# Key cache rows by VectorE block transposes, delta heads in four couples, and ScalarE row statistics in a hybrid decoder layer

## The chip, the core and the metric

One core of one Trainium2 chip runs the program. The metric is device microseconds for one execution, lower is better. TensorE is called PE here, VectorE DVE, ScalarE ACT, GpSimd POOL, and SyncE SP; all DMAs are issued from SP.

## The reference, cut to what matters

One inference step of a one-layer decoder runs over 512 prompt tokens and over 8 sequences of 4 sample tokens, 544 rows in all, width 1024. The rows are scaled and shifted by a condition, multiplied with one wide matrix (11,280 columns), and go through two branches: dilated softmax attention (three groups of eight heads of 64) and a gated delta rule (eight heads of 128, chunks). The branch outputs are gated, merged, multiplied with `w_out`, and normalised per row. The new key and value rows are outputs too.

```python
gate, (qa, ka, va, za, qkv_b, zb, a_b, b_b, ga, gb) = layer_front(x, c, w_cond, b_cond, w_in)
for gi, (window, dil) in enumerate(A_GROUPS):        # ((128,1),(512,4),(2048,16))
    o, l = dilated_prompt(qa[:, :, gi], ka[:, :, gi], va[:, :, gi], window, dil, biases[gi])
    kv_new.append(jnp.stack([ka[:, :, gi], va[:, :, gi]], axis=2)[:, seq - min(window, seq):])
state, o_b = delta_branch(qkv_ext, a_b, b_b, state0, conv_w, a_log, dt_bias)
r = (ALPHA * x + gate[:, None] * (merged @ w_out)).astype(jnp.float32)
mu = jnp.mean(r, axis=-1, keepdims=True)
var = jnp.mean(jnp.square(r - mu), axis=-1, keepdims=True)
return ((r - mu) * lax.rsqrt(var + LN_EPS)).astype(dtype) * ln_g + ln_b
```

## The kernel before, in words

Products are computed at high precision from two rounded parts of each factor: a weight tile `wt` of 128 columns is split into `hi` (ACT, a copy with rounding) and `lo` (DVE, the difference), and so is the input (`hhi`, `hlo`). Each product takes three matmuls per slice of 128 features, so a job of one weight tile is 2 halves x 8 slices x 3 = 48 matmuls of 128x272. These are the groups `pp<-hhi,hi`, `pp<-hhi,lo` and `pp<-hlo,hi`, and `stream` (line 1041) issues them job after job. The list `jobs` (from line 2152) holds the order: for each of four head pairs `j` nine attention jobs (q, k and v of three groups `g`), then jobs of the delta heads (`conv_job`), then the gates `za`, `zb`, `gb`, `ga`.

Everything else on PE is placed between those matmuls. The program does not write its engine queues by hand: a recorder notes each operation with a rank, and `schedule` orders each engine's queue with a cost table and data dependencies. All operations are issued from one line of `emit`, which is why every row of the profile says L727. Each engine works through its queue in order.

The places that the change and the prediction's steps touch:

- `shape_constants` (line 79) packs constant tables. `cst` is the first of them: the 128x128 identity used for PE transposes, a selector `selc`/`selg`, and two masks. Its DMA stands second after the first weights of the condition product (`cond_block`), which uses only the selector.
- `prompt_attention` (from line 1563) waits for q, k and v of one (j, g). It turns v into rows `vrow` by four PE transposes (`pg<-cst,spare`), and k into rows by four more (`pg<-cst,k`; one for g = 0). A copy by ACT takes k's rows from PSUM into a tile of the two-buffer tag `spare`, and DMAs with packets of 512 bytes store them to `out_kv_p`. The layout of k in SBUF is feature by time; in groups 1 and 2 time is stored in an order (r, a, n) of the dilation.
- `TOGETHER` (line 42) groups delta heads. For one group, `delta_blocks` inverts 16x16 blocks by a loop of small DVE operations (`tmp`, `Tb`), and `delta_rule` merges them up to 128x128 with six rounds of small matmuls on parts of the PE array (32x32 and 64x64). The inversion issues as many DVE instructions for one head as for two, and each round visits PE once per group. Before, head 0 and head 7 are groups of their own.
- `sample_prep` starts when head 7's convolution is done and contains one long DVE reciprocal, `kq`.
- At the end four token tiles `tt` of 128 rows are multiplied with `w_out` in two column halves `n`. DVE scales the product (`r<-pp,gp`), adds the residual (`r<-r,xr`), and takes row statistics with `bn_stats` and `bn_aggr`; `norm_out` (line 2332) then subtracts the mean and multiplies with the gain (`r<-r,mv,lng`), takes a reciprocal, and applies the factor and the offset (`r<-r,mv,lnb`, twice).

Of the kernel before, what the change touches and what calls it, by code (L numbers as in the profile page):

```python
# [11 lines left out]
F32 = mybir.dt.float32  # L12
F32R = mybir.dt.float32r
AF = mybir.ActivationFunctionType
# [26 lines left out]
S0B = 7  # L41
TOGETHER = ((0,), (1, 2), (3, 4), (5, 6), (7,))
IDLE = (8, 2, 5)
# [35 lines left out]
def shape_constants():  # L79
# [26 lines left out]
    cols, blobs = {}, []  # L106
    for names in (("ident", "selc", "selg", "low16", "dmask"), ("selab", "sel16", "triu", "btri", "bones"),
                  ("strict4", "dmask_s", "bmask"), ("hmask",), ("quarter",)):
# [671 lines left out]
def body(ctx, tc, io):  # L780
# [33 lines left out]

    cst = consts.tile([128, CONST[0].shape[1]], F32, name="cst")
    tables = {"early": cst}

# [46 lines left out]
    def to_features(pv, k, rows):  # L864

        for i in range(4):
            pe.matmul(pv[:, k + i, 0:9], rows[:, 128 * i:128 * i + 128], C("selc"), start=True, stop=True)

# [16 lines left out]
    early_ = op.tile([128, NT], F32, name="cg", tag="o")  # L885
    n = CONST[1].shape[1]
    tables["g"] = early_[:, 0:n]
# [7 lines left out]
    with ExitStack() as fctx:  # L895
# [35 lines left out]
        def cond_block(part, at, m, other):  # L931
# [19 lines left out]
            with rec.together():  # L951
                for i in range(m):
                    pe.matmul(pv[:, i, 0:9], Y[:, 128 * i:128 * i + 128], C("selc"), start=True, stop=True)
                turn_over(idle[2])
# [54 lines left out]
        with rec.together():  # L1009
            for t in range(4):  # L1010
                m = 128 if t < 3 else 16
                pe.matmul(pv[0:m, 16 * t:16 * t + 9], Y[:, 128 * t:128 * t + m], C("selc"), start=True, stop=True)
        ve.tensor_copy(shifts[:, 0:3], pv[:, 0:48].rearrange("p (a b) -> p a b", b=16)[:, :, 0:9])
# [549 lines left out]
    def prompt_attention():  # L1563

        for j in range(4):
            qt, kt, vrow = {}, {}, {}
            for g in range(3):
                yield ready[j, g]
                qt[g], kt[g], vt = (pairs[j][s, g] for s in range(3))
                vrow[g] = ap.tile([128, 4, 128], F32, name="vrow", bufs=3)  # L1570
                pt = pg()
                for i in range(4):
                    pe.transpose(pt[:, 128 * i:128 * i + 128], vt[:, 128 * i:128 * i + 128], ident)
                rec.either(vrow[g], cols128(pt))
                krow = cols128(spare()[:, :SEQ])
                pt = pg()
                i0 = 3 if g == 0 else 0
                for i in range(i0, 4):
                    pe.transpose(pt[:, 128 * i:128 * i + 128], kt[g][:, 128 * i:128 * i + 128], ident)
                rec.either(krow[:, i0:], cols128(pt)[:, i0:])  # L1580
                cs_ = slice(128 * j, 128 * j + 128)
                for u, t in enumerate((krow, vrow[g])):
                    if g == 0:
                        sp.dma_start(io["kv0_p"][:, u, cs_], t[:, 3])
                    else:
                        o = io[f"kv{g}_p"].rearrange("(n a r) u c -> a n r u c", a=4, r=4)
                        for a in range(4):
                            sp.dma_start(o[a, :, :, u, cs_], t[32 * a:32 * a + 32])

# [137 lines left out]
    def sample_decays(nd):  # L1727

        tables["d"] = d0.tile([128, CONST[2].shape[1]], F32, name="cd")
        sp.dma_start(tables["d"], io["const_d"])  # L1730
# [393 lines left out]
    def gate_rows():  # L2124

        sel = cst[:, CCOLS["selc"][0]:CCOLS["selc"][0] + 73]
        yield gates_over
# [36 lines left out]
    jobs += [za_job(j) for j in range(2)] + [zb_job(h, True) for h in range(2)] + [za_job(j) for j in range(2, 4)]  # L2164
# [148 lines left out]
    r = [o1.tile([128, D if tt < 4 else 256], F32, name=f"r{tt}") for tt in range(5)]  # L2313
    bn = [o1.tile([128, 4 if tt == 3 else 2, 6], F32, name=f"bn{tt}") for tt in range(5)]
    parts = lambda k: ((mhi[k], 0), (mhi[k], 1), (mlo[k], 0))
# [28 lines left out]
    def samples_out():  # L2344
# [13 lines left out]
        ve.tensor_add(q, q, xr)  # L2358
        ve.bn_stats(bn[4][:, 0, :], q)
        mv = o2.tile([128, 4], F32, name="mv")  # L2360
        ve.bn_aggr(mv[:, 0:2], bn[4][:, 0, :])
        pm = pd()
# [12 lines left out]
    for n in range(2):  # L2375
        if n:
            samples_out()
        for tt in range(4):
            xr, q = load_x(tt, n), r[tt]
            step = 256 if tt == 3 else 512  # L2380
            for c in range(512 * n, 512 * n + 512, step):
# [4 lines left out]
                with rec.together() if at_end else nullcontext():  # L2386
                    ve.scalar_tensor_tensor(q[:, w], po, 0.5, gp[:, w], op0=OP.mult, op1=OP.mult)
                    ve.tensor_add(q[:, w], q[:, w], xr[:, c - 512 * n:c - 512 * n + step])
                    ve.bn_stats(bn[tt][:, c // step, :], q[:, w])
                    if at_end:  # L2390
                        mv = o2.tile([128, 4], F32, name="mv")
                        ve.bn_aggr(mv[:, 0:2], bn[tt].rearrange("p a b -> p (a b)"))
                rec.rank = 0
# [37 lines left out]
def lay_out(x):  # L2431
# [9 lines left out]
        "bias_s": bias_s,  # L2441
        "const": CONST[0],
        "const_g": CONST[1],
        "const_d": CONST[2],
        "const_s": CONST[3],
        "const_q": CONST[4],
        "x": rows,
# [61 lines left out]
```

## Time and profile before

| | value |
|---|---|
| median of the runs | 893.87 us |
| runs | 891.2, 893.87 and 894.52 us |
| profiled execution | 891.03 us |
| its span, first to last instruction | 889.1 us |
| mean granted PE clock | 0.996 |
| busy: PE, DVE, ACT, POOL | 98%, 73%, 51%, 8% |
| DMA queue, share of 16 engines | 77.7% |
| last matmul ends | about 878 us |

A profile row gives the engine, the operation, output and inputs by tile name, the count, the busy time, the mean duration of one, and the idle time in front of it with its releaser. A matmul's duration (about 290 ns) is its latency; in a running stream one starts every 125 ns. So the cost of a matmul is read from the starts of its neighbours, and a PE that is busy 98% of the time is a PE whose queue has almost no hole.

### The profile page before, as it was taken

To read this page: it belongs to the slowest core of one execution; us is meant where nothing else is said; L and a number is where in the kernel's file an instruction comes from. 1 tells how busy PE (TensorE), PEld (TensorE's weight loads), DVE (VectorE), ACT (ScalarE), POOL (GpSimd) and SP (SyncE) were. 2 spreads that over 40 slices of the span, in tenths; PEclk is the share of its full clock that TensorE was granted. 3 is DMA by queue.
4 is the path that set the end of the run, shared out by engine and by line. 5 is a ranking of instruction groups with operands and counts; after the bars stand their busy time and mean duration, and the time that the engine had idled before them with its cause. 6 is when DMAs were issued, how large, how long until landed. Compare 5 with 4: busy or idle time off the path is not lost.

```text
span 889.1 us, 20805 instructions
## 1 busy us (share of the span) xinstructions
PE 868.8 (98%) x8212; PEld 821.2 (92%) x8212; DVE 646.1 (73%) x1338; ACT 453.9 (51%) x1083; POOL 70.0 (8%) x173
## 2 busy tenths in 40 slices
PE   8999999999999999999999998999999999999995
PEld 7899999899999999999999897999999999999884
DVE  3675447653379997489988647556999699998558
ACT  3555378844478834579734566653442222334321
POOL 0120011100001200000200100011010000001000
PEclk9999999999999999999999999999999999999998
DMA  9965785776879788888888675659969899987963
GB/s 343 337 207 178 228 281 180 237 265 197 273 218 316 242 278 297 279 274 272 272 272 263 223 231 166 199 186 281 349 228 375 275 421 403 352 306 236 355 211 120
DMA packets 106910, 236.18 MB, mean 266 GB/s; under 512 B 30407, under 2 KB 62481, under 8 KB 104125
## 3 DMA queue, kind: packets, MB, share of 16 engines
q1 hardware_dynamic: 106812, 234.86, 77.7%
q8 instruction: 64, 1.05, 0.5%
q14 instruction: 34, 0.27, 0.1%
HBM read 218.53 MB, written 103.97 MB: 363 GB/s over the span
## 4 chain that ended last, share of the span: by engine, by line
PE 89%; ACT 3%; DMA 2%; DVE 2%; SPq 1%; issue 1%; DVEq 0%; ACTq 0%
PE pp L727 68%; PE pg L727 9%; PE pd L727 8%; PE pb L727 4%; DMA wc<-in_w_cb 2%; SPq L727 1%; ACT L727 1%; DVE r L727 1%; DMA S<-in_state_delta 1%; ACT sq L727 1%; ACT hi L727 0%; DVE lo L727 0%; DVE zt L727 0%; ACT ext L727 0%; ACT acc L727 0%
## 5 line engine op out<-in xcount | busy, mean ns | idle before, releaser
L727 PE MATMUL pp<-hhi,hi 128*128 128x272 f32 x1360 | 399.8, 294 | 2.5 <-DVE spare L727 1.5
L727 PE MATMUL pp<-hlo,hi 128*128 128x272 f32 x1360 | 400.2, 294 | 0.0
L727 PE MATMUL pp<-hhi,lo 128*128 128x272 f32 x1360 | 399.2, 294 | 0.0
L727 PEld LDWEIGHTS pp<-hhi,hi 128*128 128x128 f32 x1360 | 256.3, 188 | 5.8 <-issue 1.8
L727 PEld LDWEIGHTS pp<-hhi,lo 128*128 128x128 f32 x1360 | 256.1, 188 | 3.9 <-issue 2.7
L727 PEld LDWEIGHTS pp<-hlo,hi 128*128 128x128 f32 x1360 | 256.6, 189 | 2.5 <-issue 1.5
L727 ACT ACTIVATE hi<-wt 128x1024 fp32r<-128x1024 f32 (+1 forms) x101 | 103.7, 1026 | 162.0 <-PE pp L727 137.3
L727 DVE TENSOR_TENSOR lo<-wt,hi 128x1024 fp32r<-128x1024 f32 (+1 forms) x101 | 119.0, 1179 | 80.3 <-ACT hi L727 78.6
L727 DVE SCALAR_TENSOR_TENSOR acc<-ext,cw,acc 128x568 f32<-128x568 f32 x72 | 57.8, 803 | 1.1 <-ACT acc L727 0.4
L727 ACT ACT_TABLE_LOAD x36 | 46.2, 1283 | 2.5 <-DVE acc L727 0.9
L727 DVE TENSOR_TENSOR slab<-slab 128x512 f32<-128x512 f32 (+1 forms) x66 | 43.1, 670 | 4.5 <-DMA slab<-in_ks 3.2
L727 DVE TENSOR_REDUCE slab<-slab 128x8 f32<-128x512 f32 (+2 forms) x66 | 42.9, 662 | 2.9 <-ACT slab L727 2.6
L727 ACT ACTIVATE zt<-pp 128x272 f32<-128x272 f32 x48 | 18.7, 390 | 41.0 <-PE pp L727 39.5
L727 PE MATMUL pp<-ybl,hi 128*128 128x272 f32 x128 | 37.0, 289 | 0.0
L727 PE MATMUL pp<-ybh,lo 128*128 128x272 f32 x128 | 37.0, 289 | 0.0
L727 PE MATMUL pp<-ybh,hi 128*128 128x272 f32 x128 | 36.8, 288 | 0.0
L727 ACT ACTIVATE P<-P,st 128x256 f32<-128x256 f32 (+1 forms) x64 | 31.1, 489 | 9.5 <-DVE st L727 8.8
L727 DVE CUSTOM_DVE_ANT_0 P<-pg,bias 128x256 f32<-128x256 f32 (+1 forms) x64 | 23.5, 402 | 13.0 <-PE pg L727 12.7
L727 POOL COPY cx<-ext 128x3 f32<-128x3 f32 (+1 forms) x48 | 22.2, 489 | 113.8 <-ACT ext L727 109.3
L727 ACT ACTIVATE spare<-pp 128x272 f32<-128x272 f32 (+1 forms) x32 | 16.2, 505 | 22.5 <-PE pp L727 22.4
L727 PEld LDWEIGHTS pp<-ybh,hi 128*128 128x128 f32 x128 | 24.2, 189 | 0.2
L727 PEld LDWEIGHTS pp<-ybl,hi 128*128 128x128 f32 x128 | 24.1, 188 | 0.2
(415 smaller groups left out, 1565.3 us busy)
## 6 DMA issues: line engine op xcount, KB each, us to landing
out_kv_s<-in_cache SPq DMA_DIRECT2D x144, 512.0 KB
wt<-in_w_in SPq DMA_DIRECT2D x85, 512.0 KB
out_kv_s<-in_cache SPq DMA_DIRECT2D x24, 496.0 KB
wc<-in_w_cb SPq DMA_DIRECT2D x16, 512.0 KB
slab<-in_ks SPq DMA_DIRECT2D x32, 256.0 KB
slab<-in_vs SPq DMA_DIRECT2D x32, 256.0 KB
kv<-in_ks SPq DMA_DIRECT2D x16, 512.0 KB
kv<-in_vs SPq DMA_DIRECT2D x16, 512.0 KB
```

The source lines that it names most:

```text
L727: getattr(real[x.engine], x.name)(*map(arg, x.args), **{k: arg(v) for k, v in x.kw.items()})
```

## The change

It does five things. The constants are split: a small table `sel` (73 columns) is loaded early, and `cst` (257 columns) after the second set of condition weights. The rows of k are made by DVE transposes of 32x32 blocks into one tile, and stored from there by four DMAs per (j, g) with packets of 128 bytes. The delta heads run in four couples, and the order of the `conv` jobs follows: head 1 goes into the first head pair, heads 6 and 7 end before the last. The tiles `tt` = 0, 1, 2 take mean and variance on ACT by two passes with an accumulator, and the DVE statistics stay for `tt` = 3 and for the sample tile.

```diff
-TOGETHER = ((0,), (1, 2), (3, 4), (5, 6), (7,))
+TOGETHER = ((0, 1), (2, 3), (4, 5), (6, 7))
...
-                sp.dma_start(cst, io["const"])
+                sp.dma_start(sel, io["const_f"])
...
         for c, m in two_by_two:
             load_cond(0, c, m)
+        sp.dma_start(cst, io["const"])
...
-                krow = cols128(spare()[:, :SEQ])
-                pt = pg()
-                i0 = 3 if g == 0 else 0
-                for i in range(i0, 4):
-                    pe.transpose(pt[:, 128 * i:128 * i + 128], kt[g][:, 128 * i:128 * i + 128], ident)
-                rec.either(krow[:, i0:], cols128(pt)[:, i0:])
                 cs_ = slice(128 * j, 128 * j + 128)
-                for u, t in enumerate((krow, vrow[g])):
+                kb, c0 = spare()[:, :SEQ], 384 if g == 0 else 0
+                if g == 0:
+                    ve.transpose(kb[:, c0:], kt[g][:, c0:])
+                else:
+                    for r in range(4):
+                        ve.transpose(kb.rearrange("p (a r c) -> p r a c", a=4, r=4)[:, r], kt[g][:, 128 * r:128 * r + 128])
+                for a in range(4):
+                    pa, ca = slice(32 * a, 32 * a + 32), slice(128 * j + 32 * a, 128 * j + 32 * a + 32)
                     if g == 0:
-                        sp.dma_start(io["kv0_p"][:, u, cs_], t[:, 3])
+                        sp.dma_start(io["kv0_p"].rearrange("(b t) u c -> t b u c", b=4)[:, :, 0, ca],
+                                     kb[pa, c0:].rearrange("p (b c) -> p b c", b=4))
                     else:
+                        o = io[f"kv{g}_p"].rearrange("(n x) u c -> n x u c", x=16)
+                        sp.dma_start(o[:, :, 0, ca], kb[pa].rearrange("p (x c) -> p x c", x=16))
...
-    h = 1
     for j in range(4):
         nine = [attention_job(j, g, s) for g in range(3) for s in range(3)]
-        if j == 3:
-            jobs += nine[:6] + [conv_job(7, s) for s in (1, 0, 2)] + nine[6:]
-        else:
-            jobs += nine + [conv_job(h + i, s) for i in range(2) for s in (1, 0, 2)]
-            h += 2
+        if not j:
+            nine = nine[:6] + [conv_job(1, s) for s in (1, 0, 2)] + nine[6:]
+        jobs += nine + [conv_job(h, s) for h in (2 * j + 2, 2 * j + 3) if h < 8 for s in (1, 0, 2)]
...
         if mv is None:
-            mv = o2.tile([128, 4], F32, name="mv")
-            ve.bn_aggr(mv[:, 0:2], bn[tt].rearrange("p a b -> p (a b)"))
-        se.activation(mv[:, 2:3], mv[:, 1:2], AF.Sqrt, bias=eps5)
+            mv, sq = o2.tile([128, 4], F32, name="mv"), o1.tile([128, D], F32, name="sq")
+            se.activation(sq, q, AF.Copy, scale=1.0 / D, accum_out=mv[:, 0:1])
+            se.activation(mv[:, 3:4], mv[:, 0:1], AF.Copy, scale=-1.0)
+            se.activation(sq, q, AF.Square, bias=mv[:, 3:4], accum_out=mv[:, 1:2])
+            se.activation(mv[:, 2:3], mv[:, 1:2], AF.Sqrt, bias=eps5, scale=1.0 / D)
...
-                    ve.bn_stats(bn[tt][:, c // step, :], q[:, w])
+                    if tt == 3:
+                        ve.bn_stats(bn[:, c // step, :], q[:, w])
```

Where the queues differ, at three places. First PE, head pair 0, where the k and v tiles of group 1 are ready. Before:

```order
L727 MATMUL pp<-hlo,hi 128x272
L727 MATMUL pp<-hhi,lo 128x272
L727 MATMUL pg<-cst,k 128x128 x4
L727 MATMUL pp<-hhi,hi 128x272
L727 MATMUL pg<-cst,spare 128x128 x4
L727 MATMUL pp<-hlo,hi 128x272
```

Now, at the same tiles:

```order
L727 MATMUL pp<-hlo,hi 128x272
L727 MATMUL pp<-hhi,lo 128x272
L727 MATMUL pg<-cst,spare 128x128 x4
L727 MATMUL pp<-hhi,hi 128x272
L727 MATMUL pp<-hlo,hi 128x272
L727 MATMUL pp<-hhi,lo 128x272
```

The four transposes of k are gone from the PE queue; over the program 36 are, and no other PE work is added. Those of v stay.

Second DVE, around the long reciprocal `kq` of `sample_prep`. Before, it stands right ahead of the evacuation `spare<-spare,pp` of the first `za` job:

```order
L727 SCALAR_TENSOR_TENSOR S<-S,etot,pd 128x128
L727 SCALAR_TENSOR_TENSOR rn<-rn,rc 128x4
L727 RECIPROCAL kq<-kq 128x512
L727 SCALAR_TENSOR_TENSOR spare<-spare,pp 128x272
L727 RECIPROCAL rn<-rn 128x4
```

Now it stands among work of the sample attention (`slab`), ahead of a weight split `lo`, and one of the new transposes (`spare<-k`) is close by:

```order
L727 STREAM_TRANSPOSE spare<-k 128x128
L727 TENSOR_TENSOR slab<-slab 128x512 x2
L727 RECIPROCAL kq<-kq 128x512
L727 TENSOR_TENSOR vr<-pb,rc 128x512
L727 TENSOR_TENSOR lo<-wt,hi 128x1024
```

It moved by one head pair, because head 7's convolution is now done before the last nine attention jobs.

Third DVE, the end of its queue, from the first half of the last product of `tt` = 3 on (buffer numbers tell the token tiles apart: r_11292, r_11320, r_11357 are `tt` = 1, 2, 3). Before:

```order
L727 BN_STATS bn_11501<-r_11357 128x6
L727 TENSOR_TENSOR r_11320<-r_11320,xr 128x512
L727 BN_STATS bn_11494<-r_11320 128x6
L727 SCALAR_TENSOR_TENSOR r_11357<-pp,gp 128x256
L727 TENSOR_TENSOR r_11357<-r_11357,xr 128x256
L727 BN_STATS bn_11501<-r_11357 128x6
L727 BN_AGGR mv<-bn_11501 128x2
L727 BN_AGGR mv<-bn_11494 128x2
L727 SCALAR_TENSOR_TENSOR r_11357<-r_11357,mv,lng 128x1024
L727 RECIPROCAL mv<-mv 128x1
L727 SCALAR_TENSOR_TENSOR r_11320<-r_11320,mv,lng 128x1024
```

Now (r_11208, r_11243, r_11279 are `tt` = 1, 2, 3):

```order
L727 SCALAR_TENSOR_TENSOR r_11208<-r_11208,mv,lnb 128x512
L727 BN_STATS bn<-r_11279 128x6
L727 SCALAR_TENSOR_TENSOR r_11208<-r_11208,mv,lnb 128x512
L727 SCALAR_TENSOR_TENSOR r_11279<-pp,gp 128x256
L727 TENSOR_TENSOR r_11279<-r_11279,xr 128x256
L727 BN_STATS bn<-r_11279 128x6
L727 BN_AGGR mv<-bn 128x2
L727 SCALAR_TENSOR_TENSOR r_11243<-r_11243,mv,lng 128x1024
L727 SCALAR_TENSOR_TENSOR r_11279<-r_11279,mv,lng 128x1024
L727 RECIPROCAL mv<-mv 128x1 x2
```

The statistics of `tt` = 2 are gone from the stretch ahead of the last product's evacuation, the offset step of `tt` = 1 stands there instead, and the gain step of `tt` = 2 comes ahead of that of `tt` = 3.

More of the change, by code (lines that the diff above doesn't have):

```diff
@@ L106, in shape_constants @@
     cols, blobs = {}, []
-    for names in (("ident", "selc", "selg", "low16", "dmask"), ("selab", "sel16", "triu", "btri", "bones"),
+    for names in (("selc", "selg"), ("ident", "low16", "dmask"), ("selab", "sel16", "triu", "btri", "bones"),
                   ("strict4", "dmask_s", "bmask"), ("hmask",), ("quarter",)):
@@ L812, in pp @@
         return psp.tile([128, 512], F32, name="pp", tag="pp")
-    cst = consts.tile([128, CONST[0].shape[1]], F32, name="cst")
-    tables = {"early": cst}
+    sel = consts.tile([128, CONST[0].shape[1]], F32, name="sel")
+    cst = consts.tile([128, CONST[1].shape[1]], F32, name="cst")
+    tables = {"first": sel, "early": cst}
     def take(gen, n):
@@ L866, in to_features @@
         for i in range(4):
-            pe.matmul(pv[:, k + i, 0:9], rows[:, 128 * i:128 * i + 128], C("selc"), start=True, stop=True)
+            pe.matmul(pv[:, k + i, 0:9], rows[:, 128 * i:128 * i + 128], C("selc", "first"), start=True, stop=True)
     f16 = lambda t: t[:, :128].rearrange("p (a b) -> p a b", b=16)
@@ L885, in body @@
     early_ = op.tile([128, NT], F32, name="cg", tag="o")
-    n = CONST[1].shape[1]
+    n = CONST[2].shape[1]
     tables["g"] = early_[:, 0:n]
@@ L952, in cond_block @@
                 for i in range(m):
-                    pe.matmul(pv[:, i, 0:9], Y[:, 128 * i:128 * i + 128], C("selc"), start=True, stop=True)
+                    pe.matmul(pv[:, i, 0:9], Y[:, 128 * i:128 * i + 128], C("selc", "first"), start=True, stop=True)
                 turn_over(idle[2])
@@ L1011, in body @@
                 m = 128 if t < 3 else 16
-                pe.matmul(pv[0:m, 16 * t:16 * t + 9], Y[:, 128 * t:128 * t + m], C("selc"), start=True, stop=True)
+                pe.matmul(pv[0:m, 16 * t:16 * t + 9], Y[:, 128 * t:128 * t + m], C("selc", "first"), start=True, stop=True)
         ve.tensor_copy(shifts[:, 0:3], pv[:, 0:48].rearrange("p (a b) -> p a b", b=16)[:, :, 0:9])
@@ L1727, in sample_decays @@
     def sample_decays(nd):
-        tables["d"] = d0.tile([128, CONST[2].shape[1]], F32, name="cd")
+        tables["d"] = d0.tile([128, CONST[3].shape[1]], F32, name="cd")
         sp.dma_start(tables["d"], io["const_d"])
@@ L2124, in gate_rows @@
     def gate_rows():
-        sel = cst[:, CCOLS["selc"][0]:CCOLS["selc"][0] + 73]
         yield gates_over
@@ L2313, in body @@
     r = [o1.tile([128, D if tt < 4 else 256], F32, name=f"r{tt}") for tt in range(5)]
-    bn = [o1.tile([128, 4 if tt == 3 else 2, 6], F32, name=f"bn{tt}") for tt in range(5)]
+    bn, bns = o1.tile([128, 4, 6], F32, name="bn"), o1.tile([128, 6], F32, name="bns")
     parts = lambda k: ((mhi[k], 0), (mhi[k], 1), (mlo[k], 0))
@@ L2334, in norm_out @@
         if mv is None:
-            mv = o2.tile([128, 4], F32, name="mv")
-            ve.bn_aggr(mv[:, 0:2], bn[tt].rearrange("p a b -> p (a b)"))
-        se.activation(mv[:, 2:3], mv[:, 1:2], AF.Sqrt, bias=eps5)
+            mv, sq = o2.tile([128, 4], F32, name="mv"), o1.tile([128, D], F32, name="sq")
[3 more added lines that the diff above has]
+            se.activation(mv[:, 2:3], mv[:, 1:2], AF.Sqrt, bias=eps5, scale=1.0 / D)
+        else:
+            se.activation(mv[:, 2:3], mv[:, 1:2], AF.Sqrt, bias=eps5)
         ve.scalar_tensor_tensor(q, q, mv[:, 0:1], lng, op0=OP.subtract, op1=OP.mult)
@@ L2358, in samples_out @@
         ve.tensor_add(q, q, xr)
-        ve.bn_stats(bn[4][:, 0, :], q)
+        ve.bn_stats(bns, q)
         mv = o2.tile([128, 4], F32, name="mv")
-        ve.bn_aggr(mv[:, 0:2], bn[4][:, 0, :])
+        ve.bn_aggr(mv[:, 0:2], bns)
         pm = pd()
@@ L2441, in lay_out @@
         "bias_s": bias_s,
[L2442 to L2446, printed above, removed]
+        "const_f": CONST[0],
+        "const": CONST[1],
+        "const_g": CONST[2],
+        "const_d": CONST[3],
+        "const_s": CONST[4],
+        "const_q": CONST[5],
         "x": rows,
```

7 lines of the change are left out of this document (4 added, 3 removed).

## The prediction

> **What bounds the kernel now.** I read the page first: the engines' busy shares, the chain that ended last, and the groups with the wait in front of them.
>
> ```profile
> span 889.1 us, 20805 instructions
> PE 868.8 (98%) x8212; PEld 821.2 (92%) x8212; DVE 646.1 (73%) x1338; ACT 453.9 (51%) x1083; POOL 70.0 (8%) x173
> q1 hardware_dynamic: 106812, 234.86, 77.7%
> PE 89%; ACT 3%; DMA 2%; DVE 2%; SPq 1%; issue 1%; DVEq 0%; ACTq 0%
> L727 ACT ACTIVATE hi<-wt 128x1024 fp32r<-128x1024 f32 (+1 forms) x101 | 103.7, 1026 | 162.0 <-PE pp L727 137.3
> ```
>
> PE is busy 98% of the span and holds 89% of the chain. The last row says who waits for whom: ACT stands idle ahead of the weight splits for 162.0 us, and 137.3 of these end when PE gives a buffer back. So the weights run ahead of PE, not behind it, and no DMA is named. What counts is what leaves the PE queue, and where PE itself waits. The PE timeline where four transposes of k stand in the stream:
>
> ```profile
> 218.57 0.29 PE L727 MATMUL pp<-hlo,hi 128*128 128x272 f32 x1
> 218.70 0.29 PE L727 MATMUL pp<-hhi,lo 128*128 128x272 f32 x1
> 218.82 0.60 PE L727 MATMUL pg<-cst,k 128*128 128x128 f32 x4
> 219.18 0.37 PE L727 MATMUL pp<-hhi,hi 128*128 128x272 f32 x1
> 219.38 0.64 PE L727 MATMUL pg<-cst,spare 128*128 128x128 f32 x4
> ...
> L727 PE MATMUL pg<-cst,k x36: 270/272/330, 69.6 to 526.4; 128*128 128x128 f32 x36
> ```
>
> The first column is the start. Two matmuls of the stream start 0.13 us apart though each lasts 0.29, so a removed matmul gives its start interval, not its duration.
>
> **K rows off PE.** The order takes 36 transposes from PE and adds nothing there. The four above occupy 218.82 to 219.18, 0.36 us, and the matmul behind them holds its place until 219.38, 0.20 us where 0.125 is usual. That is 0.44 for four, 0.11 each: 36 x 0.11 = 4.0 us gained, all of it on the path while PE does not run into a new wait.
>
> The Trainium skill, page "TensorE: Matmul & The Clock Gate", section "Part 4: PE-mode transpose", gives about 275 ns for one such transpose inside a kernel. The trace has the same number as a duration (272), but its starts show that the next work overlaps it; by the page's figure the term would be 36 x 0.275 = 9.9 us.
>
> What replaces them is 36 block transposes on DVE, and ACT loses 12 copies. The rows nearest to them:
>
> ```profile
> L727 DVE STREAM_TRANSPOSE Xc<-Tc 128x128 f32<-128x128 f32 x2 | 0.6, 306 | 0.0
> L727 DVE STREAM_TRANSPOSE XF<-Tc 32x256 f32<-32x256 f32 x12 | 5.2, 435 | 0.2
> L727 ACT ACTIVATE spare<-pg 128x512 f32<-128x512 f32 x8 | 4.8, 602 | 0.6
> L727 DVE TENSOR_TENSOR tmp<-Ls,Tb x75: 152/199/227, 101.2 to 554.6; 64x15 f32<-64x15 f32 x6, 64x28 f32<-64x28 f32 x6, 64x39 f32<-64x39 f32 x6, 64x48 f32<-64x48 f32 x6
> 250.00:310.00 60.00, 60.00 (x586) 57.20 (x585) 55.67 (x137) 50.04 (x146) 9.77 (x23) 1.00 0.82 266
> ```
>
> The last row is a stretch of the windows view: length, then busy time of PE, PEld, DVE, ACT, POOL. A transpose costs DVE 0.306 us if it is like the first row, and up to 0.435 like the second, where the written pattern is scattered (here it is scattered too): 11.0 to 15.7 us in all. A head pair has nine of them (four for groups 1 and 2, one for group 0), 2.8 to 3.9 us in about 60 us. The fullest stretch has 60 - 55.67 = 4.3 us of DVE left, so they fit. I take nothing, and the bounds are 0 and what the rivals below price.
>
> **K stores.** 4,608 packets of 512 bytes become 18,432 of 128 bytes, 2,048 for each key tile of groups 1 and 2. Packets of that size are in the trace already: `Tc<-dtz` fetches 128 KB in pieces of 32 numbers, 1,024 of them.
>
> ```profile
> DMA packets 1083, 0.61 MB, mean 340 GB/s; under 512 B 1060, under 2 KB 1060, under 8 KB 1069
> 221.33 0.57 SPq L727 DMA_DIRECT2D wt<-in_w_in  x1
> 221.95 1.91 SPq L727 DMA_DIRECT2D out_kv_p<-spare  x4
> 217.76 1.06 ACT L727 ACTIVATE hi<-wt 128x1024 fp32r<-128x1024 f32 x1 [1.86 <-PE pp L727]
> 224.69 1.06 ACT L727 ACTIVATE hi<-wt 128x1024 fp32r<-128x1024 f32 x1 [2.21 <-PE pp L727]
> ```
>
> The first row is the DMA view of 220.8 to 222.6, nearly all small packets. With 16 engines one of them took at most 1.8 x 16 / 1083 = 0.027 us, so a key tile's store holds the queue for 2048 x 0.027 / 16 = 3.4 us. What hides it is the weights' lead. A weight tile has three buffers, splits come 6.93 us apart, and the tile asked for at 221.33 is split three splits after 217.76, at about 238.5: 17 us ahead. Between the two, one burst or two pass on the queue (3.4 to 6.8 us) beside the weight's own transfer; all key stores together add 18,432 x 0.027 / 16 - 4,608 x 0.027 / 16 = 23 us over 460 us, and the queue is free in 18% of the fullest stretch (DMA share 0.82 above). Cost 0; the issues on SP grow from 36 to 48, at 1.91 / 4 = 0.48 us each, 6 us in 460.
>
> **Four couples.** The fifth group goes: its 30 inversion operations on DVE (6.0 us at the 199 ns above), and its six rounds on PE, whose matmuls stay but whose six interruptions of the stream do not. One of them:
>
> ```profile
> 132.79 0.29 PE L727 MATMUL pp<-hhi,hi 128*128 128x272 f32 x1
> 133.01 0.68 PE L727 MATMUL pd<-XF,U 64*64 64x64 f32 x8
> 133.62 0.39 PE L727 MATMUL pp<-hlo,hi 128*128 128x272 f32 x1
> 133.85 0.29 PE L727 MATMUL pp<-hhi,lo 128*128 128x272 f32 x1
> ```
>
> The matmul in front holds 0.22 until the small ones start, the one behind 0.23, instead of 0.125 each. So an interruption costs 0.20 us, and six cost 1.2. Bounds: 0, since the couples' own rounds are longer, and 2.4, if the small ones fill up better too. DVE ends up where it was: 11.0 to 15.7 added, 6.0 removed.
>
> **The moved reciprocal.** One PE wait of before is plain:
>
> ```profile
> 537.75 3.35 DVE L727 RECIPROCAL kq<-kq 128x512 f32<-128x512 f32 x1 [1.84 <-ACT kq L727]
> 541.02 0.38 DVE L727 SCALAR_TENSOR_TENSOR spare<-spare,pp 128x272 f32<-128x272 f32 x1
> 539.45 1.28 ACT L727 ACT_TABLE_LOAD   x1
> 541.46 0.39 PE L727 MATMUL pp<-hhi,hi 128*128 128x272 f32 x1 [1.54 <-DVE spare L727]
> ```
>
> The evacuation of a product stood behind 3.35 us of reciprocal and PE waited 1.54 us for it. In the new order a weight split `lo` stands behind the reciprocal, and that has the slack of a buffer. I take 1.5 us gained; at best 3.0, if the waits that follow it go too, at worst 1.5 lost, if an evacuation meets it again at its new place.
>
> **Front and tail.** At the front PE waits for condition weights:
>
> ```profile
> 19.02 1.07 PE L727 MATMUL pb<-wc,cs 128*32 128x256 f32 x16 [1.40 <-DMA wc<-in_w_cb]
> cst<-in_const SPq DMA_DIRECT2D x1, 165.0 KB
> GB/s 0 134 290 327 294 351 413 416 421 420 424 406 417 419 417 420 419 421 418 423 421 404 423 415 419 194 45 268 161 97 101 171 446 229 383 352 358 27 11 0
> ```
>
> Of 330 columns 257 move behind the weights: 165 KB x 257 / 330 = 128 KB less in front, at the 420 GB/s of the rows' plateau 0.3 us (0 if another load takes the place).
>
> ```profile
> 877.49 0.68 DVE L727 TENSOR_TENSOR r<-r,xr 128x512 f32<-128x512 f32 x1
> 878.20 0.69 DVE L727 BATCH_NORM_STATS2 bn<-r 128x6 f32<-128x512 f32 x1
> 878.81 0.41 DVE L727 SCALAR_TENSOR_TENSOR r<-pp,gp 128x256 f32<-128x256 f32 x1
> 880.17 0.33 DVE L727 BATCH_NORM_AGGREGATE mv<-bn 128x2 f32<-128x24 f32 x2
> 878.00:889.00 11.00, 0.00 (x0) 0.00 (x0) 7.68 (x15) 0.48 (x2) 0.00 (x0) 0.71 0.32 120
> ```
>
> PE's last matmul ends at about 878; then DVE has 7.68 us of work in 11. Behind the last evacuation (878.81) the list stays, but for one of two aggregations, 0.17. Ahead of it the residual and statistics of `tt` = 2 (0.68 + 0.69) make room for the two offset halves of `tt` = 1 (1.41), so the place is as full as before; but DVE comes to it with six statistics less (6 x 0.69 = 4.1 us), and may start the evacuation when the product is there, up to 0.8 earlier since PE has nothing after 878.0. I take 0.17 and a third of 0.8, 0.4 gained: bounds 1.0, and 1.1 lost if ACT's mean and variance come late (two passes over 1024 columns like the split's 1.06 each, an estimate of 3 us with the small steps between, where the sum of `tt` = 2 is ready at 878.2 and its gain step stands right behind the aggregation at 880.2).
>
> **The sum.** -4.0 - 1.2 - 1.5 - 0.3 - 0.4 = -7.4 us. The profiled execution took 891.03 us, its span 889.1; 891.03 - 7.4 = 883.6. The median of the runs, 893.87, lies 2.84 above it, so the forecast is 883.6 + 2.84, **886.5 us**. With the terms at their ends: -4.0 - 2.4 - 3.0 - 0.3 - 1.0 = -10.7 and -4.0 + 1.5 + 1.1 = -1.4, that is 883.2 to 892.5; most of the likeliest case lies in 882 to 889.4, with the runs' own scatter at the low end.
>
> **Rivals.** A measurement of this kernel tells about 0.5%, 4.5 us, from no change: faster is below 889.4, slower above 898.3.
>
> *No difference.* Four couples start later than single heads, since both convolutions must be done, and a couple's inversion may now fall into the fullest stretch. Then DVE has there 9 x 0.435 + 6.0 = 9.9 us more where 4.3 are free, the split `lo` falls behind by 5.6, and PE waits for it once: 886.5 + 5.6 = 892.1. For it: DVE works its queue in order and the stretch is 93% full. Against it: the weights' lead takes part of a lag up.
>
> *Slower, by DVE.* The same in all four head pairs: 4 x 5.6 = 22 us, 886.5 + 22.4 = 908.9. It decides from the point where what is added in a pair exceeds what DVE has free in it. Against it: DVE is 73% busy over the span, and 4.3 us is the least that I saw free.
>
> *Slower, by the stores.* If a 128 byte packet written to memory costs more than one read, the burst delays the weights. It decides when burst and transfers outlast the lead: 17 us x 16 / 2048 = 0.13 us a packet, five times the 0.027 above. At 0.16 each of eight tiles gives 20.5 - 17 = 3.5 us of wait: 886.5 + 28 = 914.5. The Trainium skill, page "DMA: Bandwidth & Descriptors", section "Specifications", says that transfers under 512 bytes are not at line rate, because the engine reads, modifies and writes. By that rule this rival holds from some factor on; the trace so far shows small reads only.
>
> **Chances.** Forecast 0.67: the PE terms are counted, and nothing is added to PE. No difference 0.22. Slower 0.11, 0.07 by DVE and 0.04 by the stores. The range 882 to 895 takes in the likeliest case with its bounds and the single DVE wait with the runs' scatter of about 3 us, and leaves the slower cases out.
>
> **What would show it.** Right: no row `pg<-cst,k`, PE busy shorter by about 5 us with as few waits as before, no wait of 1.5 us ahead of an evacuation `spare`, PE's last matmul near 871 on a profiled run and about 10.5 us behind it. Wrong: idle time ahead of PE's matmuls put down to DVE `lo` (the DVE rivals), or ahead of ACT's `hi<-wt` put down to a DMA (the stores); the duration of `spare<-k` above 0.435 us; a tail longer than 11 us with DVE waiting for ACT's statistics.

## The result, and the profile after

| | before | changed |
|---|---|---|
| median of six runs | 893.07 us | 887.38 us |
| lowest and highest | 891.2, 894.52 us | 884.89, 889.61 us |
| profiled execution, its span | 891.03, 889.1 us | 887.88, 886.1 us |

The ratio is 0.9942, with a 95% interval of 0.9924 to 0.9961: 5.7 us faster, 0.58%. The two profiles differ by 3.0 us of span only, since the profiled execution of before is below all six of its runs and that of the changed kernel a little above its median. Where a term is under 2 us, the profiles can show its place but not the sum.

The page of the changed kernel, the same rows as before:

```profile
span 886.1 us, 20733 instructions
PE 864.7 (98%) x8176; PEld 818.1 (92%) x8176; DVE 643.4 (73%) x1330; ACT 451.7 (51%) x1073; POOL 68.7 (8%) x167
q1 hardware_dynamic: 120972, 234.86, 79.0%
PE 82%; DMA 6%; DVE 5%; ACT 5%; issue 1%; SPq 1%; POOL 0%; DVEq 0%; ACTq 0%
```

PE has 36 instructions less, its busy time is 4.1 us shorter, and it is as full as before. The chain that ended last has changed: 89% PE has become 82%, and DMA has gone from 2% to 6%. So more of the chain now runs through transfers that somebody waits for. PE's own waits in the changed kernel (engine, tile, releaser: total, times, longest):

```profile
PE pd L727 <- issue: 1.5, 1, 1.5
PE pb L727 <- DMA wc<-in_w_cb: 1.1, 1, 1.1
PE pg L727 <- ACT P L727: 1.0, 1, 1.0
PE pb L727 <- DVE NTs L727: 1.0, 2, 0.5
PE pb L727 <- DMA S<-in_state_delta: 0.9, 1, 0.9
```

The wait of 1.5 us on `spare` behind the reciprocal is gone, but four rows of 0.9 to 1.5 us that were absent or shorter before have come: those on `issue` (no releaser in the profile), `P`, `NTs` and `S`. The row on `wc` was longer before, 2.0 us. All rows of PE's waits together make about 9.9 us, before 8.9. The new operations and the end of the kernel:

```profile
L727 DVE STREAM_TRANSPOSE spare<-k x36: 260/271/306, 66.4 to 518.1; 128x128 f32<-128x128 f32 x36
517.51 0.89 DVE L727 STREAM_TRANSPOSE spare<-k 128x128 f32<-128x128 f32 x4
...
L727 SPq DMA_DIRECT2D out_kv_p<-spare x48: 315/618/2976, 67.2 to 521.6; - x48
...
875.66 0.41 DVE L727 SCALAR_TENSOR_TENSOR r<-pp,gp 128x256 f32<-128x256 f32 x1
...
875.00:886.10 11.10, 0.00 (x0) 0.00 (x0) 7.37 (x14) 2.00 (x5) 0.00 (x0) 0.73 0.38 142
```

A transpose takes 0.27 us, four in a row 0.89, less than either bound of the prediction. An issue of a key store takes 0.62 us in the median; before it was 0.43:

```profile
L727 SPq DMA_DIRECT2D out_kv_p<-spare x36: 315/430/1150, 70.5 to 529.2; - x36
```

From the last evacuation to the end it is 886.1 - 875.66 = 10.4 us, before 889.1 - 878.81 = 10.3: the tail gave nothing.

### The profile page after: what moved, and what is told of

The parts are those of the page before. It is cut to its first block, busy times and chain, and to the rows that moved or that the text cites. A ratio compares the mean times of both kernels' runs of the same rounds, so it can differ in the third digit from the quotient of the medians.

```text
span 886.1 us, 20733 instructions
## 1 busy us (share of the span) xinstructions
PE 864.7 (98%) x8176; PEld 818.1 (92%) x8176; DVE 643.4 (73%) x1330; ACT 451.7 (51%) x1073; POOL 68.7 (8%) x167
## 4 chain that ended last, share of the span: by engine, by line
PE 82%; DMA 6%; DVE 5%; ACT 5%; issue 1%; SPq 1%; POOL 0%; DVEq 0%; ACTq 0%
PE pp L727 62%; PE pg L727 9%; PE pd L727 7%; PE pb L727 4%; DMA wc<-in_w_cb 2%; ACT L727 1%; DVE r L727 1%; DMA slab<-in_ks 1%; DMA dO<-orow 1%; DMA S<-in_state_delta 1%; DMA wv<-dw 1%; ACT hi L727 1%; DMA out_kv_s<-in_cache 1%; SPq L727 1%; ACT sq L727 1%
## 5 line engine op out<-in xcount | busy, mean ns | idle before, releaser
L727 PEld LDWEIGHTS pp<-ybh,lo 128*128 128x128 f32 x128 | 24.2, 189 | 0.1
```

The source lines that it names most:

```text
L727: getattr(real[x.engine], x.name)(*map(arg, x.args), **{k: arg(v) for k, v in x.kw.items()})
```

## The experiments

Twelve kernels were run in three groups, each beside runs of the kernel before on the same chip. "Order kept" below means that the planner is given the old operations and lays out all queues, and that only afterwards some operations are left out or replaced, each at its place. A re-planned kernel has a new order on every engine. The kernels with 512 byte packets move as many bytes as the others but write the blocks of the key rows of groups 1 and 2 in the wrong places. In some of the edited kernels the line of `emit` has moved, so that their rows say L730 or L728.

| label | median, us | ratio to before, 95% interval |
|---|---|---|
| e1_krows_alone | 902.28 | 1.0117 (1.0095 to 1.0138) |
| e2_couples_alone | 894.34 | 1.0021 (1.0000 to 1.0043) |
| e3_stats_alone | 891.46 | 0.9994 (0.9979 to 1.0010) |
| e4_packets_512 | 888.83 | 0.9966 (0.9946 to 0.9986) |
| e5_order_kept | 897.85 | 1.0052 (1.0034 to 1.0070) |
| e6_order_kept_512 | 893.30 | 1.0009 (0.9986 to 1.0032) |
| e7_after_512 | 883.70 | 0.9902 (0.9879 to 0.9926) |
| e8_after_again | 887.52 | 0.9941 (0.9918 to 0.9964) |
| e9_packets_64 | 893.62 | 1.0025 (1.0012 to 1.0038) |
| e10_krows_alone_512 | 897.69 | 1.0072 (1.0059 to 1.0084) |
| e11_quadrants | 892.09 | 1.0006 (0.9990 to 1.0023) |
| e12_krows_couples | 892.57 | 1.0009 (0.9993 to 1.0026) |

**Each part alone.** e1 takes the edit of `prompt_attention` and nothing else, e2 the edit of `TOGETHER` and of the job order, e3 that of the statistics.

Shortened:

```diff
 e1: the lines of prompt_attention as in the change
 e2: -TOGETHER = ((0,), (1, 2), (3, 4), (5, 6), (7,))
     +TOGETHER = ((0, 1), (2, 3), (4, 5), (6, 7)), and the new loop over jobs
 e3: the lines of norm_out, and bn_stats for tt == 3 alone
```

> The kernel before, with the key rows alone changed: 36 block transposes on DVE, 128 byte stores, the 36 PE transposes gone. Theory (PE is the pace, each transpose gone gives its start interval of 0.11 us): 4.0 us faster than before, ratio about 0.9955, the wait of 1.5 us ahead of the evacuation spare still there. Rival (DVE or the small packets take it back): 0 to 2 us faster, ratio 0.998 to 1.000, with new waits of PE on DVE or on instructions while a key store runs.

> The kernel before, with four couples and the new order of the convolution jobs alone. Theory: 1.2 us from six interruptions less and 1.5 us from the moved reciprocal, 2.7 us faster, ratio about 0.997; the profile has no wait of 1.5 us ahead of spare. Rival (the waits come back elsewhere, since couples start later): within 1 us of before, ratio 0.999 to 1.001, with other waits of the same sum.

> The kernel before, with the row statistics of three output tiles on ACT alone. The prediction's term: 0.4 us faster. Since seen in the changed kernel: from PE's last matmul to the end 11.14 us in both profiles, so rival: no difference, ratio 0.999 to 1.001, the stretch behind PE's last matmul 11.1 us.

None of the parts is faster beyond its interval. The key rows alone are 10 us slower, beyond the rival's price; the couples alone are 2 us slower where 2.7 us of gain was expected, though the wait on `spare` is gone from that profile as it should be; the statistics alone make no difference. Together the three would be 12 us slower, and with the split constants the changed kernel is 5.7 us faster. The parts do not add. The waits of PE in e1, about 17.6 us in all its rows, show where much of the time went. Most have nothing to do with key rows, which points to the new order:

```profile
PE pp L727 <- DVE zt L727: 3.4, 5, 1.8
PE pd L727 <- DVE ys L727: 2.0, 2, 1.4
PE pg L727 <- issue: 2.0, 1, 2.0
PE pb L727 <- DVE vns L727: 1.9, 1, 1.9
...
650.00:655.00 5.00, 1.51 (x9) 1.11 (x9) 4.96 (x9) 3.04 (x5) 0.00 (x0) 0.80 1.03 345
655.00:660.00 5.00, 4.72 (x20) 4.03 (x21) 3.03 (x8) 2.71 (x7) 2.71 (x6) 0.52 0.58 237
```

Key stores end long before (the last is issued at 520.6), yet at 650 to 655 DVE is busy for 4.96 us of five, PE for 1.51, and PE waits for `ys` and `vns` of the sample heads, which stand in DVE's queue behind long operations. In the last row PE works again, and its granted clock (behind the five engines) is 0.52.

**The packets, with the plan of the changed kernel.** e4 stores the key tiles by 36 DMAs with packets of 512 bytes and is planned anew; e7 does it with every instruction in its place (shortened):

```diff
 e7, groups 1 and 2:
-  sp.dma_start(o[:, :, 0, ca], kb[pa].rearrange("p (x c) -> p x c", x=16))
+  op = sp.dma_start(...)                          # planned as this
+  op.args = (o[a, :, :, 0, cs_], cols128(kb)[pa]) # issued as this
```

> The changed kernel with the same DVE transposes, but its key tiles stored by 36 DMAs with packets of 512 bytes; the key rows written are not the key rows (blocks stand in the wrong places), nothing else is left out. Theory (the packets are hidden behind the weights' lead): as the changed kernel, 0.994 of before, within 1 us. Rival (the bursts of 128 byte packets hold instructions or loads up, and PE with them): 1.5 to 3 us faster than the changed kernel, 0.991 to 0.9925 of before, and no wait of PE for issue while a key store runs.

> The changed kernel with the same queues, instruction by instruction, but packets of 512 bytes in the key stores of groups 1 and 2; the key rows of groups 1 and 2 written are not the key rows. Theory: as the changed kernel, within 1 us. Rival (packets cost): 1.5 to 3 us faster than the changed kernel.

> The changed kernel again on the chip of these runs, for comparison. Ratio to before 0.992 to 0.996 as measured first. If the 1.5 us for which PE waited for issue near 520 us was chance, the profile has it at another place or not at all.

e4 lies between the changed kernel and before, at 0.9966, where neither the theory nor the rival had put it, and tells nothing of packets, because its order is another one: its profile has three waits of PE of 2.4, 2.2 and 1.5 us, where the changed kernel's longest is 1.5. e7 does tell: 883.70 us against 887.52 in e8, the same program with other packets, on the same chip, 3.8 us faster. The intervals of the two ratios overlap by 0.0008, the runs by 0.65 us (882.79 to 885.44 and 884.79 to 888.81). So the 128 byte packets cost about 4 us. The theory of e7, that they are hidden, missed. (e7 is not free of waits: its longest, at 412.24 with no releaser shown, is 2.41 us.)

**The key rows, with the plan of before.** e5 plans the kernel before and then leaves out the 32 PE transposes and 8 copies of groups 1 and 2 and puts DVE transposes where the copies stood; e6 is e5 with packets of 512 bytes. Shortened:

```diff
     for i in range(i0, 4):
-        pe.transpose(pt[...], kt[g][...], ident)
+        op = pe.transpose(pt[...], kt[g][...], ident)
+        if g: op.swap = ()                                  # left out
-    rec.either(krow[:, i0:], cols128(pt)[:, i0:])
+    op = rec.either(krow[:, i0:], cols128(pt)[:, i0:])
+    if g: op.swap = [four DVE transposes of kt[g] into krow]
```

> The kernel before with the key rows of groups 1 and 2 made by DVE transposes and stored with 128 byte packets, but planned as if nothing had changed: 32 PE transposes and 8 copies are taken out of the queues after the plan is made, the 32 DVE transposes stand where the copies stood, and every other instruction keeps its place. Theory (a transpose off PE is worth its start interval, and what made the key rows alone slower is the new order): 32 x 0.11 = 3.5 us faster than before, ratio 0.996. Rival (the DVE transposes or the packets themselves cost PE time): 5 to 10 us slower than before, as with the key rows alone, ratio above 1.005.

> The same kernel with its key rows stored by packets of 512 bytes, every instruction in the same place; the key rows of groups 1 and 2 written are not the key rows. Theory (the packets are hidden): as the run with 128 byte packets, within 1 us. Rival (packets cost): faster than it by 1.5 us or more.

Both theories missed, and both rivals came: e5 is 5.6 us above before, and e6 is 4.5 us faster than e5. e6 has 32 transposes less on PE, 32 more on DVE and 8 copies less, everything else in place, and is not faster than before (1.0009). PE in e6, at the tile of group 1 that the prediction shows at 218.57, and ACT beside it:

```profile
217.26 0.29 PE L730 MATMUL pp<-hhi,lo 128*128 128x272 f32 x1
217.39 0.29 PE L730 MATMUL pp<-hhi,hi 128*128 128x272 f32 x1
217.93 0.66 PE L730 MATMUL pg<-cst,spare 128*128 128x128 f32 x4 [0.25 <-ACT vs L730]
218.34 0.37 PE L730 MATMUL pp<-hlo,hi 128*128 128x272 f32 x1
...
217.30 0.58 ACT L730 ACTIVATE spare<-pp 128x240 f32<-128x240 f32 x1
217.67 0.23 ACT L730 ACTIVATE vs<-pp 128x32 f32<-128x32 f32 x1
```

The transposes of v need what ACT has just evacuated. In the old order those of k stood ahead of them and filled that time. Without them PE stands idle instead: from the matmul of the stream ahead of v's transposes to the one behind them it is now 218.34 - 217.39 = 0.95 us. In before it was 219.78 - 219.18 = 0.60, by this row and one that the prediction shows:

```profile
219.78 0.37 PE L727 MATMUL pp<-hlo,hi 128*128 128x272 f32 x1
```

The four transposes gave 0.35 at their own place (219.18 - 218.70 = 0.48 became 217.39 - 217.26 = 0.13), and this wait took it. The whole stretch, from 218.70 to 219.78 before and from 217.26 to 218.34 in e6, is 1.08 us in both. Four more of the eight places of groups 1 and 2 are like this one, equal to 0.02 us; at the other three e6 gains 0.1 to 0.4 us. In the changed kernel v's transposes wait nowhere. At one of its places, with ACT's evacuation last:

```profile
374.45 0.29 PE L727 MATMUL pp<-hlo,hi 128*128 128x272 f32 x1
374.58 0.60 PE L727 MATMUL pg<-cst,spare 128*128 128x128 f32 x4
374.94 0.37 PE L727 MATMUL pp<-hhi,lo 128*128 128x272 f32 x1
...
373.84 0.58 ACT L727 ACTIVATE spare<-pp 128x240 f32<-128x240 f32 x1
```

v's transposes start 0.74 us behind the start of ACT's evacuation, where e6 has 0.63 (217.93 - 217.30) with PE idle; the planner has put them further back, behind matmuls of the stream. Their stretch takes 0.49 us, and at five other places 0.47 or 0.48 (of the last two, one has twelve score matmuls ahead of v's transposes). Against the 1.08 of before, which holds one more matmul of the stream (0.125), 1.08 - 0.125 - 0.49 = 0.47 us are gone for four transposes, 0.12 each. So a transpose off PE is worth its start interval only where other work takes its place as cover.

e5 is 4.5 us slower than e6 by the medians (their ranges overlap, 893.1 to 899.2 and 890.2 to 899.6; the intervals of their ratios do not). The same place in e6 and in e5, SP's issues first (the second number is the time that the issue took), then ACT and PE:

```profile
220.51 2.20 SPq L730 DMA_DIRECT2D out_kv_p<-spare  x4
222.81 3.17 SPq L730 DMA_DIRECT2D out_kv_p<-vrow  x4
229.05 1.03 SPq L730 DMA_DIRECT2D slab<-in_bias_s  x2
...
233.67 0.50 ACT L730 ACTIVATE slab<-slab 128x352 f32<-128x352 f32 x1 [3.56 <-DMA slab<-in_bias_s]
...
234.71 1.11 PE L730 MATMUL pd<-U,NTs 64*64 64x64 f32 x16 [0.39 <-ACT U L730]
```

```profile
222.04 2.79 SPq L730 DMA_DIRECT2D out_kv_p<-spare  x4
224.93 4.62 SPq L730 DMA_DIRECT2D out_kv_p<-vrow  x4
231.46 1.03 SPq L730 DMA_DIRECT2D slab<-in_bias_s  x2
...
236.72 0.50 ACT L730 ACTIVATE slab<-slab 128x352 f32<-128x352 f32 x1 [5.08 <-DMA slab<-in_bias_s]
...
237.76 1.11 PE L730 MATMUL pd<-U,NTs 64*64 64x64 f32 x16 [1.90 <-ACT U L730]
```

Read from top to bottom: the key store's four issues take 2.79 us where they took 2.20, and the value store behind it, whose packets have not changed, takes 4.62 where it took 3.17. A load of a bias table stands behind both in SP's queue. From the start of the key store its issue comes 0.9 us later than in e6 (231.46 - 222.04 = 9.42, 229.05 - 220.51 = 8.54), and ACT, which waits for that load with `U` of the delta heads behind it in its own queue, waits 1.5 us longer. PE's round of small matmuls needs `U` and waits 1.90 us for 0.39. No weight is late here.

**More packets, and the key rows alone with fewer.** e9 issues each key store as two DMAs of 64 byte packets; e10 is e1 with 512 byte packets. Shortened:

```diff
 e9:  -  one DMA of kb[pa], packets of 32 numbers
      +  op.instead = two DMAs of kb[pa][:, :, 0:16] and [:, :, 16:32]
 e10: the edit of e7, on e1
```

> The changed kernel, every instruction in its place, but each key store of groups 1 and 2 is issued as two DMAs with packets of 64 bytes: 16,384 packets of 128 bytes become 32,768, and 32 issues on SP become 64. Theory (the stores hold up SP and the short transfers behind them, and through these ACT, DVE and PE): 3 to 8 us slower than the changed kernel, about 891 to 896 us, with new waits of PE on ACT or DVE shortly behind a key store. Rival (what the 512 byte runs gained was chance or HBM noise): as the changed kernel, within 1.5 us.

> The kernel before with the key rows alone changed, in the same queues as that run, but with packets of 512 bytes in the key stores of groups 1 and 2; the key rows of groups 1 and 2 written are not the key rows. Theory (of the 10 us that the key rows alone lost, about 4 belong to the packets and the rest to the new order of the queues): 896 to 900 us, 5 us or so slower than before, with the waits near 650 us still there. Rival (it is all the packets): 888 to 890, 3 to 4 us faster than before.

Both came out as the theory has it. e9 is 0.84% above e8 by the ratios, 7.5 us, with twice the packets and twice the issues. One of its new waits stands behind key stores (SP, then DVE and PE):

```profile
268.38 0.63 SPq L728 DMA_DIRECT2D out_kv_p<-spare  x1
269.72 1.25 SPq L728 DMA_DIRECT2D out_kv_p<-spare  x2
272.94 0.38 SPq L730 DMA_DIRECT2D slab<-in_ks  x1
...
278.11 0.69 DVE L730 TENSOR_TENSOR slab<-slab 128x512 f32<-128x512 f32 x1 [2.60 <-DMA slab<-in_ks]
279.44 0.35 DVE L730 SCALAR_TENSOR_TENSOR Tc<-pd,cst,Tc 128x128 f32<-128x128 f32 x1
...
279.84 0.69 PE L730 MATMUL pd<-Tc,NTs 32*32 32x32 f32 x32 [2.05 <-DVE Tc L730]
```

DVE stands 2.60 us for a load of `slab<-in_ks`, which SP issues behind the doubled key stores. The step `Tc` of the delta heads, which PE needs, stands behind it in DVE's queue. In the changed kernel the load at the same place is issued at 268.78, and PE has no wait on `Tc`:

```profile
268.78 0.38 SPq L727 DMA_DIRECT2D slab<-in_ks  x1
```

e10 against e1: 1.0072 and 1.0117, 4.0 us for the packets once more. What is left in e10 is 6 us above before, and e6, with the old order, is 0.8 above it: the difference is the new order.

**A try to do better.** e11 keeps the changed kernel's plan, but writes each feature block of k to the quarter of the partitions in which its time stands, so that whole rows of 512 bytes can be stored. e12 takes key rows and couples without the rest. Shortened:

```diff
 e11: -  ve.transpose(kb ... [:, r], kt[g][:, 128 * r:128 * r + 128])
      +  for b in range(4): ve.transpose(kb[32 * r:32 * r + 32] ... [:, :, 32 * b:32 * b + 32],
      +                                  kt[g][32 * b:32 * b + 32] ... [:, :, 32 * r:32 * r + 32])
 e12: the edits of e1 and e2
```

> The changed kernel, every instruction in its place, but each DVE transpose of a key tile of groups 1 and 2 is issued as four of 32 partitions that write to other quarters of the tile, so that whole key rows lie in one partition and are stored with packets of 512 bytes; all outputs as the reference. Theory (the packets cost 4 us, DVE has room): as with 512 byte packets, 884 us, at most 2 us more for 96 further DVE transposes of 0.22 us, so faster than both kernels. Rival (DVE is late behind 3.5 us of transposes in a row): 888 us or more, with new waits of PE on DVE lo or spare.

> The kernel before with the key rows and the four couples, without the ACT statistics and the split constants. Theory (statistics and constants are worth under 1 us; the key rows and the couples need each other only through the order that the planner makes): within 2 us of the changed kernel, 886 to 890 us. Rival (each set of changes draws a new order, and its luck is worth more than the parts): anywhere from 885 to 900, more than 3 us from the changed kernel.

e11 went the rival's way, 892.09 us, though its long waits are on `Tc` and `vs` and not on `lo` or `spare`. Sixteen transposes of 32 partitions take 5.10 us, not 3.5, and DVE works in order:

```profile
522.54 5.10 DVE L728 STREAM_TRANSPOSE spare<-k 32x128 f32<-32x128 f32 x16
...
528.27 0.34 DVE L730 SCALAR_TENSOR_TENSOR Tc<-pd,cst,Tc 128x128 f32<-128x128 f32 x1
...
528.67 0.89 PE L730 MATMUL pd<-Tc,NTs 32*32 32x32 f32 x32 [4.44 <-DVE Tc L730]
```

One such wait of 4.4 us, with the one of 2.5 us on `vs` that the profile has elsewhere, is more than the packets had cost. The changed kernel remains the fastest here that does the whole computation. e12 is 5 to 6 us above the changed kernel (892.57 to 887.52, or 1.0009 to 0.9941), against its theory. The statistics gave nothing in e3, and the split constants, which had no run of their own, do not bring the stream forward: its first matmul starts at 39.58 in e12, at 39.95 in the changed kernel and at 39.93 in before. What is left is the order drawn with them. e12's profiled execution (889.91 us) is the third fastest of its twelve and does not show where its median loses.

## Why the prediction was right, point by point

The forecast of 886.5 us lies 0.9 us from the median, and the sign and the likeliest case held. Of the steps behind it, the work taken from PE held, one cost was left out, and the small terms can't be told from noise.

- **What bounds the kernel: right.** In all twelve runs PE is busy for 97 or 98% of the span, and time moved with PE's waits and with the stretches of low clock behind some of them (last section). But the row that I read, ACT's splits waiting for PE, speaks of weights alone. It says nothing of the transfers that do not run ahead.
- **K rows off PE, 4.0 us: right at its place in the changed kernel, nothing in e6.** The count of 36 was right, and the interval too: 0.12 us a transpose where 0.11 was forecast, at a place where v's transposes do not wait. With the old order kept, e6 gave 0 (+0.8, from -1.2 to +2.9 us), since k's transposes had covered PE's wait for v's evacuation: "all of it on the path while PE does not run into a new wait" was the condition. The changed kernel keeps it and e6 does not. The prediction did not say what would keep it. The 275 ns that the Trainium skill gives ("TensorE: Matmul & The Clock Gate", "Part 4: PE-mode transpose") made 9.9 us and was further off.
- **K stores, 0 us: wrong.** "Cost 0", hidden by the weights' lead. Measured: 3.8 us (e8 and e7), 4.5 (e5 and e6), 4.0 (e1 and e10). The weights' lead did hide them from the weights: in the changed kernel one wait of ACT ahead of `hi<-wt`, 5.78 us at 524.20, is put down to the weight's DMA (in e8 the same wait, 5.99 us, is put down to PE), but no wait of PE is put down to `hi` or `lo`. What stood behind the stores on SP were short transfers that an engine was about to need: `slab<-in_bias_s`, `slab<-in_ks`. The prediction named the queue and priced the issues as unchanged at 0.48 us each, 6 us in all; by the medians they took 0.62 each, 48 x 0.62 - 36 x 0.43 = 14 us, while the same 48 issues with 512 byte packets took 0.43 each (e7). The time of the DMA engines, which I bounded at 23 us, grew by 0.790 x 886.1 - 0.777 x 889.1 = 9 us; between kernels that differ in packets alone it grew by 0.4 us (e7, e8), 8.5 (e6, e5) and 7.1 (e10, e1). The Trainium skill's rule that transfers under 512 bytes are not at line rate ("DMA: Bandwidth & Descriptors", "Specifications") named the right transfers; the rival drawn from it, a late weight, did not hold PE up.
- **Four couples and the reciprocal, 1.2 + 1.5 us: not there alone.** The wait of 1.54 us went, in e2 and in the changed kernel, as the order had shown; e2 was 2 us slower all the same, with a wait of 2.8 us on DVE `o` that before has not.
- **DVE: right.** 0.27 us a transpose, no row of PE waits on `lo`. The bound of 0.435 was put down to a scattered write, but its row is a tile of 256 columns; the scattered write of 128 columns did not cost more. The DVE rival needed added work in one place; e11 brought it, and PE waited 4.4 us.
- **Front 0.3 and tail 0.4 us: nothing to be told from noise.** The tail is 10.4 us for 10.3, and e3 is 0.5 us faster with an interval across 0. The first matmul of the stream starts at 39.95 us for 39.93. The waits of `pb` on `wc` vary from none (e6) to 2.1 us (e5) among runs that have the same front.
- **The signs.** `pg<-cst,k` has no row and the wait on `spare` is gone, as said. PE's busy time fell by 4.1 us where "about 5" was said, with some 1.7 us of low clock in it (last section). But the waits are not as few as before (9.9 us for 8.9), and PE's last matmul ended at 875.0 and not near 871, since the profiled span fell by 3.0 us and not by 7.4.
- **The sum.** With packets of 512 bytes the changed kernel is 8.7 us faster than before (0.9902), with 128 bytes 5.2 to 5.7; forecast 7.4. So what was left out, 3.8 us, was met in part by 1.3 us more gain than the terms have. Another 0.8 us of the good hit is the base: the forecast starts from 893.87, and the median of before was 893.07 here. The same edits one by one or two by two, each planned anew, gave +10.4, +1.9, -0.5 and +0.8 us. That luck of the order, several us either way, was not a term of the sum, and it is larger than all but one of the terms. So the number was right in part by accident: a cost of 4 us was left out, and a good order was not counted on. That the changed kernel's order is a good one is inferred from the other orders' times; which of its queues makes it so is left open.

## What to carry to other kernels

When an in-order queue gets more or smaller transfers, look not at the queue's share of time but at the next short transfer behind them that an engine is about to wait for, and at what stands behind the waiting instruction on that engine. Work taken from the bounding engine pays only where nothing behind it was waiting for something else: look at the next instruction's operands before counting the start intervals. In a kernel whose order a planner makes, keep the order when a part is to be priced, because parts that are planned anew differ by more than the parts are worth.

## What the runs showed of the hardware

A wait of PE can cost more than its length. In the changed kernel PE stands 1.5 us ahead of `pd<-W,Xc` at 520.70 with nothing shown that it waits for; ACT and DVE hardly work in that window either (0.00 and 0.35 us of 2.4). Behind it the granted clock (behind the engines' columns) is about half, and matmuls of the stream start 0.23 us apart where 0.125 is usual:

```profile
519.00:521.40 2.40, 0.89 (x37) 0.77 (x26) 0.35 (x2) 0.00 (x0) 0.00 (x0) 1.00 1.13 431
521.40:525.00 3.60, 3.60 (x34) 3.35 (x33) 2.48 (x7) 0.81 (x1) 0.78 (x2) 0.53 0.69 163
522.14 0.43 PE L727 MATMUL pp<-hhi,hi 128*128 128x272 f32 x1
522.37 0.43 PE L727 MATMUL pp<-hlo,hi 128*128 128x272 f32 x1
```

At a clock of 0.53 the 3.6 us do the work of about 1.9, so by this estimate 1.7 us are lost on top of the 1.5. e1 shows the same behind its waits (0.80 and 0.52), and e9 at 283 to 286 (0.50).

Not every such wait has it. Behind the 1.54 us on `spare` in before, and behind the wait at the same instruction as above in e7, the clock is 1.00:

```profile
541.40:545.00 3.60, 2.71 (x22) 2.35 (x24) 3.31 (x8) 2.73 (x5) 0.34 (x1) 1.00 0.22 77
```

```profile
521.40:525.00 3.60, 3.60 (x56) 3.41 (x56) 3.27 (x8) 1.63 (x4) 0.78 (x2) 1.00 1.00 329
```

e3 has the wait on `spare` too, 1.53 us, with a clock of 0.50 from 543.5 to 546.5. Every stretch of low clock ahead of PE's last matmul, in all profiles, begins in a wait of PE of 1.5 us or more or within some 2 us behind it; e7's wait of 2.41 us has none. What decides is open. Summed by the same estimate over windows of 1 us, PE lost to them nothing in before, e6, e7 and e12, 1.4 to 1.7 us in the changed kernel, e3, e5, e8 and e10, 3.0 in e2, 3.3 in e11, and 5.7 to 6.6 in e1, e4 and e9. So part of what an order or a packet size cost above came by way of the clock: of the 2.7 us between the profiles of e8 and e7 1.7, of the 6.4 between e5 and e6 1.7, and of the 5.7 between e1 and e10 4.1.

The wait at 520.70 itself is not chance and not the packets: e8 has it at the same instruction, and e7, with 512 byte packets, too.

```profile
520.61 0.30 PE L727 MATMUL pd<-W,Xc 32*32 32x16 f32 x12 [1.57 <-issue]
```

```profile
520.93 0.30 PE L727 MATMUL pd<-W,Xc 32*32 32x16 f32 x12 [1.32 <-issue]
```

What PE waits for there is open; the DMA queue is full at that time (share 1.13 above).
